# Loading most constants after the first norm's factor, and a lower limit on the work issued ahead of a step, in a decoder trunk on one core

## The chip, the core and the metric

The kernel runs on one core of a Trainium2 chip. A core has a matrix engine (TensorE, PE in the profile, with its weight loads as PEld), three engines for elementwise work (VectorE, DVE; ScalarE, ACT; GpSimd, POOL), and SyncE (SP), which here only issues transfers. Each engine has a queue of its own and works through it in order; engines wait for one another by semaphores. Transfers (DMAs) are issued by SyncE, ScalarE or GpSimd and then run beside the engines.

The metric is the device time of one execution in microseconds (us). The kernel before takes 902.55 us, the median of three runs.

## What is computed

Two layers of a hybrid decoder trunk over 256 rows of 2048 numbers, in 32-bit floats. Each layer normalises its rows, multiplies them by one wide matrix, feeds four groups of heads, gates their outputs, and multiplies the result by an output matrix; a last norm ends the whole.

```python
def hybrid_layer(x, layer_idx, ...):
    h = rms_norm(x, norm_g)
    p = split_columns(jnp.einsum("bsd,de->bse", h, w_in))
    fox = forgetting_attention(...) * silu(p["fox_g"])      # softmax with a forget gate
    diff = rms_norm(differential_attention(...)) * silu(p["diff_g"])
    moba = moba_attention(...) * silu(p["moba_g"])
    gla = rms_norm(gla_chunked(...)) * silu(p["gla_g"])     # gated linear attention
    mixed = jnp.concatenate([fox, diff, moba, gla], axis=-1)
    return x + jnp.einsum("bse,ed->bsd", mixed, w_out)

def reference(x, ...):
    for l in range(DEPTH):                                  # DEPTH = 2
        x = hybrid_layer(x, l, ...)
    return rms_norm(x, final_norm_g)
```

`rms_norm` multiplies each row by 1/rms, the reciprocal root of the mean of its squares. It is the same factor for a whole row, so the kernel multiplies the rows without it first and puts the factor on the product.

## The kernel before

**Steps.** The work of TensorE is a list of steps, `plan`. A normal step multiplies both halves of the rows (2 x 128) by a slice of weights of two blocks of 128 rows, most often 512 columns wide. For accuracy each operand is split into a high part and a low part, and a step makes three products: high by high, low by high, high by low. So a normal step is 12 matmuls of 128x512, eight that need the weights' high part `hi` and four that need their low part `lo`. Eight steps make a block (a product of one column range), whose sum lies in two banks of PSUM until ScalarE or VectorE takes it out. Two of the wide products are made with fewer matmuls out of sums and differences of halves: these are the pair steps (`"pair"`), six matmuls each, some of which read sums of the normalised rows that the task `sum_forms` prepares on VectorE. They stand between the normal steps of blocks 3 to 12 of each layer.

**The loop.** The last part of `hybrid_trunk` goes over `plan` and writes every engine's queue in one order. For step i it:

- calls the results of blocks that are complete (`settle`, which calls `done`), as soon as 1/rms of the layer is known (`("r", l)` in `ready`) and a buffer is free;
- emits the high part of step i+3 on ScalarE (`prepare`);
- emits the matmuls of step i (`multiply`, `multiply_form`);
- calls `tick`, which emits other work, and
- emits the low part of step i+3 on VectorE (`complete`). SyncE then loads weights into the buffer `raw` that this frees; there are five.

There are four buffers each for `hi` and `lo`, so the parts of step i+4 wait for TensorE to have left step i.

**Other work.** Everything else (norms, attention, gates, transposes through memory and back) is written as Python generators in the list `tasks`. `tick` goes through them in the order of the list, lets each go on by up to three pieces, and stops as soon as VectorE's or ScalarE's planned end (`v_.tail`, `a_.tail`) lies more than `AHEAD` past TensorE's planned time (`times.now`). A planner, `Times` and `Timed`, keeps these: each operation of VectorE or ScalarE costs a fixed time and a time per element, a transfer made by `move` the number given with it, a transfer issued by a plain `dma_start` nothing. A task goes on only when its last result is planned within `LEAD`, 1.5 us. The planner orders the queues; it puts no waits into them. Where a step needs something that no task has emitted yet, `tick(False)` is called until it is there.

**The start.** Blocks 0 to 2 (columns of the gated linear group and a few others) are made in steps 0 to 23, chunk by chunk as the rows arrive. The generator `first_rms` squares the four chunks on ScalarE, sums them on VectorE, has TensorE sum over partitions (a matmul by `one`, side<-one,four in the profile, after step 20) and, in the same piece, emits `pw` on VectorE and the power on GpSimd that gives 1/rms (`rstd`). `know_rows` then gives out `("r", 0)`, `settle` calls `gla_first` for block 0, and only after this the high part of step 24 is emitted.

The task `constants` starts when the last chunk of rows is split. It issues all constants' loads on ScalarE's queue: `ct` (tables), the small gate matrix (`gla_wa2`, `gla_ba`, into `w3`, split into `wa`), the masks, `neg_b` (the causal mask), `gng`, `fb`, the lambdas (`lamt`) and `dng`. After them come the cast of the masks on VectorE, the split of `wa` and the products of the lambdas. `gla` waits for the key "constants".

**The end of a layer.** The groups' products go into `mTh` and `mTl` (high and low part; the profile shows `mTl<-four,mTh`), which the output projection reads group by group: the first two groups for three ranges of columns, then the third group, then the fourth.

Line 265 of the profile is the helper that emits every operation of VectorE and ScalarE, line 440 the one that emits matmuls; so groups are told apart by their tiles.

## Time and profile before

| | |
|---|---|
| runs | 902.55 us median of 3 (901.48 to 902.99) |
| the profiled execution's own time | 902.47 us |
| its span, first to last instruction | 900.7 us |
| TensorE idle in the span | 900.7 - 884.1 = 16.6 us |
| mean granted clock of TensorE | 0.996 |
| bytes moved | 227.44 MB, mean 253 GB/s |

The page's chain of work that ended last has TensorE for 88% of the span, ScalarE for 4%, transfers for 3%, VectorE for 2%. A row of the timeline gives start and length in us, engine and line, operation, the tile written and those read, the shape, how many instructions were merged, and in brackets how long the engine had been idle and what ended that. A `q` after an engine's name marks its queue: an instruction that issues a transfer or waits. A busy TensorE may still be slow; the granted clock in the view of windows tells.

### The profile page before, as it was taken

What the parts mean: (1) busy time and instruction counts of PE and PEld (TensorE: products, weight loads), DVE (VectorE), ACT (ScalarE), POOL (GpSimd) and SP (SyncE); (2) the same over time, 40 slices, a digit from 0 to 9 for tenths busy, and PEclk for the clock granted to TensorE, in tenths of its full rate; (3) what the DMA queues carried; (4) which work ended last, traced back from release to release, by engine and by line L of the source; (5) the groups of instructions that cost most, each with busy time, mean ns of one, the idle gap of its engine ahead of it and who ended that gap; (6) DMA issues with size and microseconds to landing.
All of it is one profiled execution on the core that took longest, in us unless ns stands there. A gap on an engine that the chain in (4) does not pass through costs nothing.

```text
span 900.7 us, 12457 instructions
## 1 busy us (share of the span) xinstructions
PE 884.1 (98%) x4380; PEld 751.8 (83%) x4380; DVE 662.3 (74%) x943; ACT 560.5 (62%) x846; POOL 61.7 (7%) x87
## 2 busy tenths in 40 slices
PE   9989999999999999999999989999999999999996
PEld 7977888988888888888899877898888888888886
DVE  6668989787776956666658868877767789376673
ACT  7568765686557656654746975567655476675461
POOL 1001100100010001000000010110000100011000
PEclk9999999999999999999999999999999999999999
DMA  8879987778696695887877896967959967859842
GB/s 294 280 210 304 295 245 232 239 225 320 214 277 228 230 326 158 283 311 231 280 241 274 280 317 198 255 187 294 305 200 279 286 198 226 306 186 322 327 145 95
DMA packets 84141, 227.44 MB, mean 253 GB/s; under 512 B 9979, under 2 KB 30443, under 8 KB 83950
## 3 DMA queue, kind: packets, MB, share of 16 engines
q1 hardware_dynamic: 73336, 192.00, 62.6%
q0 software_dynamic: 9152, 33.03, 14.3%
q10 hardware_dynamic: 1590, 1.62, 0.6%
q8 instruction: 34, 0.56, 0.2%
q14 instruction: 29, 0.24, 0.1%
HBM read 204.06 MB, written 22.55 MB: 252 GB/s over the span
## 4 chain that ended last, share of the span: by engine, by line
PE 88%; ACT 4%; DMA 3%; DVE 2%; issue 2%; SPq 0%; POOL 0%; POOLq 0%; DVEq 0%; ACTq 0%
PE mm L440 75%; PE side L440 13%; DMA raw<-in_weights 2%; ACT hi L265 1%; ACT L265 1%; DVE lo L265 1%; ACT four L265 1%; DVE four L265 1%; DVE tq L265 0%; DMA four<-in_xt 0%; DMA gng<-in_gla_norm_gt 0%; SPq L271 0%; ACT eight L265 0%; ACT mTh L265 0%; ACT fe L265 0%
## 5 line engine op out<-in xcount | busy, mean ns | idle before, releaser
L265 ACT ACTIVATE hi<-raw 128x1024 fp32r<-128x1024 f32 (+2 forms) x319 | 317.3, 1010 | 203.8 <-PE mm L440 118.0
L440 PE MATMUL mm<-hi,hTp 128*128 128x512 f32 (+1 forms) x1760 | 432.4, 382 | 5.3 <-ACT four L265 3.0
L265 DVE TENSOR_TENSOR lo<-raw,hi 128x1024 fp32r<-128x1024 f32 (+2 forms) x319 | 362.7, 1155 | 98.3 <-ACT hi L265 91.9
L440 PEld LDWEIGHTS mm<-hi,hTp 128*128 128x128 f32 x1760 | 323.3, 189 | 66.1 <-ACT hi L265 4.0
L440 PE MATMUL mm<-lo,hTp 128*128 128x512 f32 (+1 forms) x880 | 238.5, 381 | 3.0 <-DVE lo L265 3.0
L440 PEld LDWEIGHTS mm<-lo,hTp 128*128 128x128 f32 x880 | 162.4, 188 | 35.2 <-DVE lo L265 5.8
L440 PE MATMUL mm<-hi,mTh 128*128 128x512 f32 (+1 forms) x256 | 69.7, 379 | 0.0
L440 PE MATMUL mm<-hi,mTl 128*128 128x512 f32 (+1 forms) x256 | 69.0, 376 | 0.0
L440 PE MATMUL mm<-lo,mTh 128*128 128x512 f32 (+1 forms) x256 | 69.0, 376 | 0.0
L440 PEld LDWEIGHTS mm<-hi,mTl 128*128 128x128 f32 x256 | 46.3, 188 | 8.9
L440 PEld LDWEIGHTS mm<-lo,mTh 128*128 128x128 f32 x256 | 46.3, 188 | 8.9
L271 POOL DMA_DIRECT2D four<-far x40 | 21.9, 547 | 450.2 <-DVE lo L265 183.9
L440 PEld LDWEIGHTS mm<-hi,mTh 128*128 128x128 f32 x256 | 45.7, 188 | 8.0
L265 ACT ACTIVATE four<-mm,rstd 128x512 f32<-128x512 f32 (+2 forms) x56 | 36.6, 667 | 24.7 <-PE mm L440 24.4
L265 ACT ACTIVATE four<-four 128x512 fp32r<-128x512 f32 (+3 forms) x44 | 35.1, 816 | 16.6 <-DMA four<-far 12.1
L265 DVE STREAM_TRANSPOSE four<-four 128x1024 f32<-128x1024 f32 (+1 forms) x34 | 38.6, 1140 | 1.8 <-ACT four L265 1.8
L440 PEld LDWEIGHTS side<-four,four 128*128 128x128 f32 (+1 forms) x336 | 36.3, 190 | 2.5 <-issue 1.4
L440 PE MATMUL side<-four,four 128*128 128x128 f32 (+3 forms) x336 | 37.3, 281 | 0.0
L265 DVE TENSOR_TENSOR four<-four,four 128x512 fp32r<-128x512 f32 (+3 forms) x31 | 26.7, 883 | 9.2 <-ACT four L265 9.2
L271 POOL DMA_DIRECT2D xs<-in_weights x24 | 21.1, 879 | 177.3 <-DVE lo L265 60.2
L265 ACT ACTIVATE hi<-xs 128x1024 fp32r<-128x1024 f32 x24 | 25.4, 1058 | 8.7 <-PE mm L440 8.6
L265 DVE TENSOR_TENSOR lo<-xs,hi 128x1024 fp32r<-128x1024 f32 x24 | 29.1, 1214 | 0.5 <-ACT hi L265 0.4
(146 smaller groups left out, 674.2 us busy)
## 6 DMA issues: line engine op xcount, KB each, us to landing
raw<-in_weights SPq DMA_DIRECT2D x271, 512.0 KB, 5.2
four<-far POOLq DMA_DIRECT2D x34, 512.0 KB, 6.8
far<-four SPq DMA_DIRECT2D x128, 128.0 KB, 4.8
raw<-in_weights SPq DMA_DIRECT2D x46, 348.0 KB, 4.5
xs<-in_weights POOLq DMA_DIRECT2D x24, 512.0 KB, 7.5
xs<-in_weights SPq DMA_DIRECT2D x8, 512.0 KB, 7.1
xs<-in_x SPq DMA_DIRECT2D x4, 512.0 KB, 8.2
kept<-xs SPq DMA_DIRECT2D x1, 2048.0 KB
```

The source lines that it names most:

```text
L265: return f(*args, **kw)
L271: self.eng.dma_start(out, src, **kw)
L440: t_.matmul(out, lhsT, rhs, start=start, stop=stop, **kw)
```

## The change

Four constants change and two are new: `AHEAD` goes from 5.0 to 3.0, `ROOM` from 5.0 to 2.0; `BEFORE_LO` and `BEFORE_HI` are 1.5.

In `constants`, `ct` and the small gate matrix are loaded where they were, now with a planned time (4.5 and 5.0 us), and `wa` is split as soon as they are planned to be there. Then the task waits for `("r", 0)`. Only then are the masks loaded (planned 5.0 us), cast and given out under a key of their own, and then the lambdas, `dng`, `neg_b`, `gng` and `fb`. `gla` waits for "masks" after its scans.

In the loop, `tick` gets two limits, one for VectorE and one for ScalarE, in place of one for both and a `room` for ScalarE. `lasts(z)` is the planned length of step z. The limits are the length of the next two steps less 1.5 us, at most `AHEAD`, and for ScalarE at most `ROOM` at the last step of a block.

```diff
-AHEAD = 5.0
+AHEAD = 3.0
-ROOM = 5.0
+ROOM = 2.0
+BEFORE_LO = 1.5
+BEFORE_HI = 1.5
...
-            if v_.tail > times.now + AHEAD or a_.tail > times.now + ranks["room"]:
+            if v_.tail > times.now + ranks["v"] or a_.tail > times.now + ranks["a"]:
                 break
...
         yield from until(("h", 0, 3))
-        nc.scalar.dma_start(ct, const)
+        a_.move(ct, const, 4.5)
         w3 = s2.get([P, DEPTH, 256])
         g_.memset(w3, 0.0)
         for i in range(0, 96, 32):
             nc.scalar.dma_start(w3[i:i + 16], gla_wa2.rearrange("l r e -> r l e"))
-            nc.scalar.dma_start(w3[i + 16:i + 17].rearrange("p l e -> p (l e)"), gla_ba.rearrange("(o l) e -> o (l e)", o=1))
-        yield
+            a_.move(w3[i + 16:i + 17].rearrange("p l e -> p (l e)"), gla_ba.rearrange("(o l) e -> o (l e)", o=1), 5.0)
+        yield
+        hi_of(wa, w3)
+        yield
+        lo_of(wa[64:96], w3[64:96], wa[64:96])
+        s2.put(w3)
+        given_out("constants")
+        yield from until(("r", 0))
         c, n = CAT["masks"]
         mb = s4.get([P, n], BF16)
-        nc.scalar.dma_start(mb, const_b[:, c:c + n])
-        yield
+        a_.move(mb, const_b[:, c:c + n], 5.0)
+        yield
+        v_.tensor_copy(masks.rearrange("p l t -> p (l t)"), mb)
+        s4.put(mb)
+        given_out("masks")
+        lamt = s2.get([P, DEPTH, 4, 64])
+        a_.move(lamt.rearrange("p l a d -> p (l a d)"), bcast_rows(diff_lam, 0, DEPTH * 256), 5.0)
+        nc.scalar.dma_start(dng, diff_norm_gt)
         c, n = CAT["neg"]
         nc.scalar.dma_start(neg_b, const_b[:, c:c + n])
         nc.scalar.dma_start(gng, gla_norm_gt)
         nc.scalar.dma_start(fb.rearrange("p l h -> p (l h)"), bcast_rows(fox_fb, 0, DEPTH * H))
-        yield
-        lamt = s2.get([P, DEPTH, 4, 64])
-        nc.scalar.dma_start(lamt.rearrange("p l a d -> p (l a d)"), bcast_rows(diff_lam, 0, DEPTH * 256))
-        nc.scalar.dma_start(dng, diff_norm_gt)
-        yield
-        v_.tensor_copy(masks.rearrange("p l t -> p (l t)"), mb)
-        s4.put(mb)
-        hi_of(wa, w3)
-        yield
-        lo_of(wa[64:96], w3[64:96], wa[64:96])
-        s2.put(w3)
-        given_out("constants")
         yield
...
         s2.put(gl)
+        yield from until("masks")
         yield from until(("gla_qk", l))
...
+    def lasts(z):
+        return 1.36 if "pair" in z else len(z["kts"]) * (z["block"]["n"] + 32) / 400.0
...
-        ranks["room"] = ROOM if s["last"] else AHEAD
+        soon = sum(lasts(z) for z in plan[i + 1:i + ahead])
+        ranks["v"] = min(AHEAD, soon - BEFORE_LO)
+        ranks["a"] = min(AHEAD, soon - BEFORE_HI, ROOM if s["last"] else AHEAD)
         tick()
-        ranks["room"] = AHEAD
+        ranks["v"] = ranks["a"] = AHEAD
```

## The prediction

> **What bounds the kernel now.** I read the page first, for the share of each engine.

> ```profile
> span 900.7 us, 12457 instructions
> PE 884.1 (98%) x4380; PEld 751.8 (83%) x4380; DVE 662.3 (74%) x943; ACT 560.5 (62%) x846; POOL 61.7 (7%) x87
> ```

> TensorE is the bound: 16.6 us of the span are not its own (900.7 - 884.1), and no edit of this change removes a matmul. So the most that can be won is in the places where TensorE waits or runs slowly. The view of waits, for PE alone, names them:

> ```profile
> PE mm L440 <- DVE lo L265: 3.0, 4, 1.4
> PE mm L440 <- ACT four L265: 3.0, 2, 2.3
> PE mm L440 <- ACT hi L265: 2.2, 1, 2.2
> ```

> These are 8.2 us in seven waits: four for a step's low part, two for a bank that ScalarE had not emptied, one for a high part. The rest of the 16.6 us is mostly start and end. The busy time hides one more loss, which the view of windows shows beside the single wait for a high part:

> ```profile
> 58.50:61.00 2.50, 0.28 (x3) 0.00 (x1) 0.02 (x1) 2.49 (x6) 1.04 (x1) 1.00 0.80 213
> 61.00:65.00 4.00, 4.00 (x11) 3.13 (x12) 4.00 (x4) 4.00 (x9) 0.00 (x0) 0.57 0.95 217
> ```

> The columns are stage and length, then busy us of PE, PEld, DVE, ACT and POOL, the granted clock, the DMA share and GB/s. PE did nothing from 58.78 to 61.00, and then "busy" for 4.00 us at a clock of 0.57: 0.43 x 4.00 = 1.72 us lost. The wait and its slow restart cost 2.22 + 1.72 = 3.94 us. The timeline tells why the high part came late:

> ```profile
> 43.22 1.06 ACT L265 ACTIVATE hi<-raw 128x1024 fp32r<-128x1024 f32 x1 [2.17 <-PE side L440]
> 45.04 0.35 ACTq L552 DMA_DIRECT2D four<-in_const_b  x1
> 45.43 0.68 ACTq L555 DMA_DIRECT2D neg_b<-in_const_b  x1
> 46.64 0.33 ACTq L556 DMA_DIRECT2D gng<-in_gla_norm_gt  x1
> 47.01 0.44 ACTq L557 DMA_DIRECT2D fb<-in_fox_fb  x1
> 47.49 0.59 ACTq L560 DMA_DIRECT2D four<-in_diff_lam  x1
> 48.13 0.51 ACTq L561 DMA_DIRECT2D dng<-in_diff_norm_gt  x1
> 48.22 0.48 PE L440 MATMUL mm<-lo,hTp 128*128 128x348 f32 x2
> 48.69 1.06 ACT L265 ACTIVATE four<-four 128x1024 f32<-128x1024 f32 x1 [4.41 <-DMA gng<-in_gla_norm_gt]
> 51.12 1.44 ACT L265 ACTIVATE hi<-raw 128x696 fp32r<-128x696 f32 x2
> 51.53 0.58 PE L440 MATMUL side<-one,four 128*128 128x1 f32 x4
> 55.41 0.87 DVE L265 TENSOR_TENSOR lo<-raw,hi 128x696 fp32r<-128x696 f32 x1
> 56.20 0.15 DVE L265 TENSOR_SCALAR pw<-side 128x2 f32<-128x2 f32 x1
> 56.51 0.71 POOL L265 TENSOR_TENSOR rstd<-pw,halfpow 128x2 f32<-128x2 f32 x1 [52.80 <-DVE pw L265]
> 58.30 0.48 PE L440 MATMUL side<-lo,hTp 128*128 128x348 f32 x2
> 59.88 1.06 ACT L265 ACTIVATE hi<-raw 128x1024 fp32r<-128x1024 f32 x1
> 61.00 2.00 PE L440 MATMUL mm<-hi,hTp 128*128 128x512 f32 x4 [2.22 <-ACT hi L265]
> ```

> ScalarE is through with a high part at 44.28 and then issues six loads of constants until 48.64; only then comes the last square of the first norm (48.69), and behind it the high parts of steps 21 to 23. So the low part of step 23 is done at 56.28, the power's input `pw`, emitted behind it, at 56.35, and 1/rms at 57.22. The results of block 0 need 1/rms, stand ahead of step 24's high part on ScalarE, and that part ends at 60.94: TensorE, free since 58.78, starts at 61.00.

> **The change part by part.**

> *Constants after 1/rms.* The six issues (0.35 + 0.68 + 0.33 + 0.44 + 0.59 + 0.51 = 2.90 us, 4.36 us from 44.28 to 48.64 with their waits) leave that place; so do the cast of the masks and the work on the lambdas on VectorE. The seven loads of `ct` and `wa`'s source stay, ahead of the high part at 43.22, which waits for TensorE anyway. The square can then start at 44.3 instead of 48.69. What is late next? Step 23's high part needs the buffer of step 19, which TensorE leaves at 48.70 (48.22 + 0.48): it runs from 48.7 to 49.5, the low part until 50.4. `pw` also needs the matmul of the sums, which ends at 52.11 by its place between steps 20 and 21. So `pw` moves from 56.20 to about 52.2, and 1/rms from 57.22 to about 53.2. Step 24's high part ended 60.94 - 57.22 = 3.72 us after it; now at 56.9, ahead of 58.78 by 1.9 us. The wait of 2.22 us goes, and with it the slow clock: **-3.9 us**. Bounds: at least 0 (1/rms no earlier), at most these 3.94.

> What comes back: one load is issued a step later and five some 3.5 us after that (the planner now counts 5.0 us for them), between the high parts of steps 26 and 27. That puts 0.35 and 2.55 us into ScalarE's queue, ahead of the results of block 2 and of high parts. Its cover is this idle time, which shows that it had caught up:

> ```profile
> 67.71 1.06 ACT L265 ACTIVATE hi<-raw 128x1024 fp32r<-128x1024 f32 x1 [0.33 <-PE mm L440]
> 70.62 1.06 ACT L265 ACTIVATE hi<-raw 128x1024 fp32r<-128x1024 f32 x1 [1.85 <-DMA raw<-in_weights]
> ```

> That is 2.18 us against 2.90, with the high parts some 2 steps early, so I cost it at nothing; without the cover it is 0.7 us, and up to 3.6 us (48.64 - 45.04) if the issues wait again. The added waits: the cast of the masks waits on VectorE for its load, with the low part of step 26 queued behind it and TensorE behind that; `gla` waits for "masks" after its scans (85.06 below), long after the cast, at no cost. The loads of weights move too: SyncE issues one when a low part has freed its buffer, and so sooner wherever a low part comes sooner.

> At this place the clock is the larger unknown. The row shows that 2.22 us without matmuls were followed by a clock of 0.57. [...]

> *Work ahead limited.* Ticks emit other work until VectorE's or ScalarE's planned end is 5.0 us past TensorE's. Now it is 3.0 us, or less: two coming steps of 512 columns last 2.72 us each (5.44 - 1.5 = 3.94, so 3.0 holds), with a pair step among them 1.36 + 2.72 - 1.5 = 2.58, and ScalarE has 2.0 at a block's end. No instruction is added or removed; lows and highs come sooner in their queues, and the rest later. The longest of the four waits for a low part shows what it could do:

> ```profile
> 82.50 0.17 DVE L265 SCALAR_TENSOR_TENSOR fz<-fx,fe 128x8 f32<-128x8 f32 x1 [2.35 <-ACT fe L265]
> ...
> 83.92 1.22 DVE L265 TENSOR_TENSOR four<-four,hTp 128x1024 f32<-128x1024 f32 x1
> 85.06 1.36 DVE L265 TENSOR_TENSOR_SCAN four<-one,four 128x128 f32<-128x128 f32 x4
> 86.34 2.33 DVE L265 TENSOR_TENSOR lo<-raw,hi 128x1024 fp32r<-128x1024 f32 x2
> 87.59 0.73 PE L440 MATMUL mm<-lo,hTp 128*128 128x512 f32 x2 [1.43 <-DVE lo L265]
> ```

> VectorE idles 2.35 us for ScalarE, then does a sum and four scans (1.22 + 1.36) ahead of a low part that is 1.43 us late. A limit of 2.58 may send the scans behind that low part, 1.36 of the 1.43 us; the idle 2.35 us, a dependency that the planner times too early, remains. So I take half of the waits for low parts, 1.5 of 3.0 us: **-1.5 us**. Bounds: -6.0 (those and the waits for banks all gone) and +3.0 (as many new ones of the same size). The longer wait for a bank stays, since it hangs on a load:

> ```profile
> 531.73 1.06 ACT L265 ACTIVATE hi<-raw 128x1024 fp32r<-128x1024 f32 x1 [0.30 <-DMA raw<-in_weights]
> 532.69 1.25 ACT L265 ACTIVATE four<-mm,r0.125_4134 128x512 f32<-128x512 f32 x2
> 533.41 1.21 PE L440 MATMUL mm<-hi,hTp 128*128 128x512 f32 x4 [2.28 <-ACT four L265]
> ```

> *Sum*, against the profiled execution's own 902.47 us (span 900.7 and 1.8 around it; the median of the runs is 902.55, 0.1 more): 902.5 - 3.9 - 1.5 = **897.1 us**, rounded to 897.0.

> **The rivals.**

> *Only the early part counts.* The limits move waits about without reducing their sum. For it: the waits come from ScalarE's and the loads' real lateness, which the planner does not see. 902.5 - 3.9 = 898.6.

> [...]

> *The gain is handed on.* Everything runs 4 us earlier into a stage (80 to 85 us below) where ScalarE and the loads are full; five issues add 2.55 us and TensorE waits there instead. Against it: in 50 to 55 us the loads were nearly idle for want of low parts, so they can move up too.

> ```profile
> 50.00:55.00 5.00, 4.93 (x25) 3.79 (x24) 4.83 (x10) 2.56 (x4) 0.00 (x0) 1.00 0.31 83
> 80.00:85.00 5.00, 5.00 (x23) 4.01 (x23) 2.62 (x5) 4.97 (x6) 0.85 (x1) 1.00 1.06 407
> ```

> With 2.55 given back and the limits worth nothing: 902.5 - 3.9 + 2.55 = 901.1.

> *Slower: work held back misses the output projection.* Group products enter it in a fixed order, and the second and third groups come late:

> ```profile
> 383.74 1.23 DVE L265 TENSOR_TENSOR mTl<-four,mTh 128x1024 fp32r<-128x1024 f32 x1 [4.32 <-ACT mTh L265]
> 392.12 1.07 PE L440 MATMUL mm<-hi,mTh 128*128 128x512 f32 x4
> 402.49 1.23 DVE L265 TENSOR_TENSOR mTl<-four,mTh 128x1024 fp32r<-128x1024 f32 x1
> 410.80 1.07 PE L440 MATMUL mm<-hi,mTh 128*128 128x512 f32 x4
> ```

> They are ready 7.15 us (392.12 - 384.97) and 7.08 us (410.80 - 403.72) ahead. The limits hold back just this work. If a chain comes over 7.1 us later, TensorE waits; at 10 us, four times over two layers, 4 x 2.9 = 11.6 us: 902.5 - 5.4 + 11.6 = 908.7. Against it: the queues are not full all the time (VectorE 74%), and a shorter queue also lets a chain's next link start sooner.

> *The change does not do what it says*: 1/rms stays where it is, since `pw` stays behind the low part of step 23 for another reason (a load, or the constants' waits): 902.5 - 1.5 = 901.0.

> **How the numbers follow.** Chances: forecast 0.60, only the early part 0.13, slow clock 0.04, handed on 0.10, slower 0.08, 1/rms not earlier 0.05. The range reaches from 892.0 (3.9 and all 6.0 us gone is 892.6) to 902.0 (3.9 won, 3.0 lost to new waits, is 901.6). It leaves out the slower rival and the tails of the others, some 0.15. A difference of 0.2%, 1.8 us, is about what a measurement of this kernel can tell from none: faster is below 900.7. There lie the forecast, the two rivals near 898.7 and half of the one handed on: 0.82. Within: the other half and the last rival, 0.10. Slower: 0.08.

> **What would show it.** Right: in the changed profile ScalarE's square stands near 44.5, `pw` near 52.2, `rstd` ends near 53.2; no wait of PE for a high part at 58.8 and a granted clock of 1.00 in 61 to 65; the five issues stand after 60 us with no wait of PE within 5 us; PE's waits for low parts sum to about 1.5 us, those for banks still to some 3. Wrong: `rstd` near 57, or a wait between 60 and 90 us longer than 1.43; waits for a new cause after 100 us that add up to over 3 us; or the last `mTl` of a group within a step of its use.

## The result and the profile after

The changed kernel takes **906.93 us** (median of 9 runs, 904.77 to 910.15) against 902.66 us for the kernel before (9 runs, 900.64 to 903.50): a ratio of 1.0053, with a 95% interval of 1.0035 to 1.0071. The forecast was 897.0 us, with a range up to 902.0. It went the other way. The profiled span is 4.5 us longer (905.2 against 900.7).

The first lines of the page of the changed kernel (share of each engine), and then the view of waits for PE alone:

```profile
span 905.2 us, 12467 instructions
...
PE 885.9 (98%) x4380; PEld 752.4 (83%) x4380; DVE 662.6 (73%) x943; ACT 558.7 (62%) x846; POOL 60.4 (7%) x87
```

```profile
PE mm L442 <- ACT mTh L267: 5.2, 2, 2.9
PE mm L442 <- ACT hi L267: 3.1, 1, 3.1
PE mm L442 <- DVE lo L267: 1.8, 6, 0.4
...
PE mm L442 <- ACT hTp L267: 0.4, 1, 0.4
```

The number of matmuls is the same. Of the waits of before, those for low parts fell from 3.0 to 1.8 us, those for banks (3.0) and the one for a high part near 60 us (2.2) are gone. In their place stand two waits for `mTh`, the part of a group's result that enters the output projection, one for another high part, and a short one (0.4) for split rows (`hTp`) near the start. The view of windows shows the two places of the old loss and two new ones (columns as before):

```profile
61.00:65.00 4.00, 4.00 (x19) 3.31 (x18) 3.97 (x7) 3.00 (x4) 0.00 (x0) 1.00 0.87 313
...
390.40:393.80 3.40, 3.40 (x9) 2.43 (x8) 3.40 (x4) 3.40 (x6) 0.00 (x0) 0.51 0.42 159
...
540.60:544.00 3.40, 3.40 (x10) 2.62 (x9) 3.16 (x11) 3.40 (x9) 0.00 (x0) 0.50 0.52 186
```

The clock is full where it was 0.57. But behind two of the new waits it is halved for 3.40 us: 0.49 x 3.40 = 1.67 and 0.50 x 3.40 = 1.70 us lost.

**The account.** Won: the wait and the slow clock near 60 us (2.2 + 1.7), low parts 3.0 - 1.8 = 1.2, banks 3.0; together 8.1 us. Lost: `mTh` 5.2, a high part 3.1, slow clock 1.7 + 1.7; together 11.7. Net 3.6 of the 4.5 us by which the span grew. The wait for `hTp` adds 0.4, and the stretch from TensorE's last matmul to the end of the span another 0.4 (7.4 us before, 7.7 after), which leaves 0.1.

**The early part, step by step.** The timeline of the changed kernel, against the lines around 50 us shown in the prediction:

```profile
44.83 1.05 ACT L267 ACTIVATE four<-four 128x1024 f32<-128x1024 f32 x1
...
51.77 0.16 DVE L267 TENSOR_SCALAR pw<-side 128x2 f32<-128x2 f32 x1 [0.50 <-PE side L442]
...
52.08 0.70 POOL L267 TENSOR_TENSOR rstd<-pw,halfpow 128x2 f32<-128x2 f32 x1 [48.38 <-DVE pw L267]
...
55.45 1.07 ACT L267 ACTIVATE hi<-raw 128x1024 fp32r<-128x1024 f32 x1
...
58.27 1.08 PE L442 MATMUL mm<-hi,hTp 128*128 128x512 f32 x4
...
63.05 0.35 ACTq L273 DMA_DIRECT2D four<-in_diff_lam  x1
...
67.23 0.33 ACTq L571 DMA_DIRECT2D fb<-in_fox_fb  x1
...
102.75 0.61 PE L442 MATMUL mm<-hi,mTh 128*128 128x512 f32 x2
```

The square starts at 44.83 (48.69 before), `pw` at 51.77 (56.20), 1/rms ends at 52.78 (57.22), step 24's high part ends at 56.52 (60.94), and TensorE starts the step at 58.27 with no wait. The last five issues lie on ScalarE's queue between 63.05 and 67.56, which is 4.5 us with their waits; TensorE did not stop there. At the first pair step that multiplies by the sums TensorE is 6.4 us ahead of the kernel before:

```profile
109.16 0.62 PE L440 MATMUL mm<-hi,mTh 128*128 128x512 f32 x2
```

**Where it is lost.** The second group's results reach the output projection by a long chain: products on TensorE, results stored by SyncE and fetched by GpSimd, work of ScalarE and VectorE between them, at the end a scale by `dng` and the split into `mTh` and `mTl`. First the kernel before in the timeline: one set of products in the middle of the chain, the last products, the first matmul of the first group's projection (which belongs to TensorE's fixed order and serves as a mark), and `mTh`:

```profile
294.15 1.69 PE L440 MATMUL side<-four,four 64*128 64x256 f32 x24
...
349.86 1.59 PE L440 MATMUL side<-four,four 128*128 128x256 f32 x12
...
359.48 0.61 PE L440 MATMUL mm<-hi,mTh 128*128 128x512 f32 x2
...
382.64 1.06 ACT L265 ACTIVATE mTh<-four 128x1024 fp32r<-128x1024 f32 x1
```

The same in the changed kernel, with the two uses that waited:

```profile
294.25 1.69 PE L442 MATMUL side<-four,four 64*128 64x256 f32 x24
...
353.25 0.62 PE L442 MATMUL mm<-hi,mTh 128*128 128x512 f32 x2
...
358.69 1.60 PE L442 MATMUL side<-four,four 128*128 128x256 f32 x12
...
386.44 1.07 PE L442 MATMUL side<-lo,mTh 128*128 128x512 f32 x4
387.54 1.15 ACT L267 ACTIVATE four<-four,dng 128x1024 f32<-128x1024 f32 x1 [6.77 <-DMA four<-far]
388.71 1.06 ACT L267 ACTIVATE mTh<-four 128x1024 fp32r<-128x1024 f32 x1
389.82 1.57 PE L442 MATMUL mm<-hi,mTh 128*128 128x512 f32 x4 [2.31 <-ACT mTh L267]
...
838.78 1.20 PE L442 MATMUL mm<-hi,mTh 128*128 128x512 f32 x4 [2.85 <-ACT mTh L267]
```

TensorE passes the mark 6.2 us sooner (353.25 against 359.48), but the products of the middle are no sooner and the last ones 8.8 us later. Against the mark, the last products go from 9.6 us ahead of it (359.48 - 349.86) to 5.4 us behind it. `mTh` ends at 383.70 in the kernel before, 8.4 us ahead of its use at 392.12; here at 389.77, 2.3 us after TensorE was free (387.51). The chain has slipped by **10.7 us** against TensorE. Of this, TensorE's being earlier at the use is 4.6 us (392.12 against 387.51), and `mTh`'s being later is 6.1 us. The same wait comes in the second layer at 838.78.

The wait for a high part is of another kind. It lies some 90 us into the second layer, whose first product TensorE starts at 448.36. The timeline of the changed kernel there:

```profile
538.14 1.06 ACT L267 ACTIVATE four<-four 128x1024 f32<-128x1024 f32 x1 [5.07 <-DMA four<-far]
539.11 1.04 ACT L267 ACTIVATE hi<-raw 128x1024 fp32r<-128x1024 f32 x1
...
540.20 1.32 PE L442 MATMUL mm<-hi,hTp 128*128 128x512 f32 x3 [3.12 <-ACT hi L267]
```

The high part stands on ScalarE behind an operation that waited 5.07 us for a fetch; TensorE waits behind both. In the kernel before, the last operation of that form ahead of `four<-ct,dgs` waits for nothing and runs 13 us sooner:

```profile
524.73 1.04 ACT L265 ACTIVATE four<-four 128x1024 f32<-128x1024 f32 x1
```

In the kernel before TensorE stops a few steps ahead of this place, for the bank of 533.41 that the prediction shows (2.28 us, at full clock behind it). So 2.3 of the 3.0 us won at banks and the loss of 3.1 + 1.7 us at the high part belong to one stretch of the second layer, which as a whole lost.

### The profile page after: what moved, and what is told of

Same layout as the page of the kernel before. It is cut to its first block, busy times and chain, and to the rows that moved or that the text cites. A ratio compares the mean times of both kernels' runs of the same rounds, so it can differ in the third digit from the quotient of the medians.

```text
span 905.2 us, 12467 instructions
## 1 busy us (share of the span) xinstructions
PE 885.9 (98%) x4380; PEld 752.4 (83%) x4380; DVE 662.6 (73%) x943; ACT 558.7 (62%) x846; POOL 60.4 (7%) x87
## 4 chain that ended last, share of the span: by engine, by line
PE 81%; DMA 7%; DVE 5%; issue 5%; ACT 1%; POOL 0%; POOLq 0%; SPq 0%; ACTq 0%; DVEq 0%
PE mm L442 70%; PE side L442 11%; DMA four<-far 3%; DMA raw<-in_weights 2%; DVE lo L267 2%; DMA far<-four 1%; DVE four L267 1%; DVE mx L267 1%; DVE tq L267 0%; DVE mTl L267 0%; ACT hi L267 0%; ACT four L267 0%; ACT mTh L267 0%; DMA neg_b<-in_const_b 0%; DVE side L267 0%
## 5 line engine op out<-in xcount | busy, mean ns | idle before, releaser
L267 DVE TENSOR_TENSOR mTl<-four,mTh 128x1024 fp32r<-128x1024 f32 x16 | 19.5, 1220 | 17.7 <-ACT mTh L267 17.7
```

The costliest lines, as they stand in the source:

```text
L267: return f(*args, **kw)
```

## The experiments

Theory A, formed from these views: the limits of 3.0 us and less hold back the chains, and everything that was lost is lost there, while the constants' part brings what was forecast. Its first rival: the moved constants are the cause. The expectations name the theories and their numbers for each run. All times are medians in us; the ratio is to the kernel before in the same set of runs, over all of its runs and so not exactly that of two medians (902.34 for E1 to E4, 902.10 for E6, E7, E8 and E10, 902.65 for E11 to E13), with its 95% interval.

| run | what it is | time | ratio | interval |
|---|---|---|---|---|
| E1 | constants moved, old limits | 904.72 | 1.0036 | 1.0022 to 1.0051 |
| E2 | new limits, constants as before | 911.32 | 1.0090 | 1.0076 to 1.0104 |
| E3 | limit of 3.0 alone | 920.69 | 1.0215 | 1.0195 to 1.0236 |
| E4 | limit by coming steps alone | 913.14 | 1.0115 | 1.0097 to 1.0132 |
| E13 | ScalarE's 2.0 at a block's end alone | 913.16 | 1.0121 | 1.0100 to 1.0142 |
| E6 | new limits until step 59 only | 898.89 | 0.9958 | 0.9945 to 0.9971 |
| E7 | new limits from step 60 only | 915.02 | 1.0146 | 1.0125 to 1.0168 |
| E8 | E1, the sums given out one by one | 901.22 | 0.9989 | 0.9976 to 1.0002 |
| E10 | change, old limits in steps 100 to 151 | 898.19 | 0.9950 | 0.9938 to 0.9961 |
| E11 | change, old limits in steps 100 to 111 | 900.39 | 0.9983 | 0.9965 to 1.0000 |
| E12 | change, old limits in steps 122 to 151 | 913.94 | 1.0127 | 1.0107 to 1.0147 |

### E1 and E2: the two parts apart

E1 sets `AHEAD` and `ROOM` back and takes out the limit by coming steps:

```diff
-        soon = sum(lasts(z) for z in plan[i + 1:i + ahead])
-        ranks["v"] = min(AHEAD, soon - BEFORE_LO)
-        ranks["a"] = min(AHEAD, soon - BEFORE_HI, ROOM if s["last"] else AHEAD)
+        ranks["v"], ranks["a"] = AHEAD, ROOM if s["last"] else AHEAD
```

> The constants' part of the change alone; the limits on work ahead are those of before (5.0 us for both engines). Theory A (the lower limits stretch the chain of the second group, differential attention, until the output projection waits for it): TensorE's waits for mTh near 387 and 836 us are gone, the gain at 58 to 65 us stays, and the time is 895 to 898. Theory B (TensorE, being some 6 us earlier, outruns a chain that takes as long as before; the limits matter little): the waits for mTh stay, 4 to 6 us in sum, and the time is 903 to 907.

The waits for `mTh` are gone, as theory A has it, but the time, 904.72, is far above what it gave. Its timeline, and then its window at the longest wait:

```profile
108.57 4.19 DVE L267 TENSOR_TENSOR tq<-eight,four 64x128 f32<-64x128 f32 x14
112.77 1.22 DVE L267 TENSOR_TENSOR mTl<-four,mTh 128x1024 fp32r<-128x1024 f32 x1
113.91 1.50 DVE L267 TENSOR_TENSOR eight<-eight,four 128x128 f32<-128x128 f32 x7
115.33 1.22 DVE L267 TENSOR_TENSOR lo<-xs,hi 128x1024 fp32r<-128x1024 f32 x1
116.60 1.22 PE L442 MATMUL mm<-lo,mTh 128*128 128x512 f32 x2 [3.68 <-DVE lo L267]
```

```profile
116.60:120.00 3.40, 3.40 (x8) 2.72 (x9) 3.34 (x6) 1.06 (x1) 0.87 (x1) 0.51 0.41 70
```

VectorE works through 4.19 + 1.22 + 1.50 us of other work ahead of one low part; TensorE waits 3.68 us and then runs 3.40 us at a clock of 0.51. In the code this is the place where the first pair step finds the sums that it needs not yet planned: the loop then calls `tick(False)`, which moves the planned time on by 0.3 us a call, until all that is missing is emitted, and only then goes on to the step; so the limits no longer hold this work back. So theory A failed as to the constants: with the old limits, moving them makes the kernel slower.

E2 puts `constants` back as it was (and `gla` without the wait for "masks") and keeps the new limits:

```diff
         yield from until(("h", 0, 3))
-        a_.move(ct, const, 4.5)
+        nc.scalar.dma_start(ct, const)
...
-        yield from until("masks")
         yield from until(("gla_qk", l))
```

> The lower limits alone; the constants are loaded and used as before the change. Theory A: the chain of the second group ends three steps (8.2 us) later against TensorE, so the waits for mTh are there in both layers, and the wait near 58 us is back: 908 to 912. Theory B: no waits for mTh, since TensorE is no earlier than before: 901 to 903.

The time, 911.32, is within theory A's range. The view of waits of E2 (its profiled execution took 915.74 us, the longest of the five):

```profile
PE mm L442 <- ACT mTh L267: 5.9, 2, 3.9
```

The waits for `mTh` are there without any move of a constant: the moved constants don't cause them.

### E3, E4 and E13: the limits one at a time

E3 keeps `AHEAD = 3.0` alone (`ROOM = 5.0`, and no limit by coming steps):

```diff
-        soon = sum(lasts(z) for z in plan[i + 1:i + ahead])
-        ranks["v"] = min(AHEAD, soon - BEFORE_LO)
-        ranks["a"] = min(AHEAD, soon - BEFORE_HI, ROOM if s["last"] else AHEAD)
+        ranks["v"] = ranks["a"] = AHEAD
```

> The constants' part with the flat limit of 3.0 us alone: no limit from the coming steps, none of its own for ScalarE at a block's end. Theory A: the queues' order puts the second group's last parts five steps later than with 5.0 us, so the waits for mTh are longer than in the changed kernel: 6 us or more in each layer, 909 to 914. Theory B: as the changed kernel, 905 to 908.

E4 keeps the limit by coming steps alone (and issues `fb` together with the masks):

```diff
-AHEAD = 3.0
+AHEAD = 5.0
-ROOM = 2.0
+ROOM = 5.0
...
         a_.move(mb, const_b[:, c:c + n], 5.0)
+        nc.scalar.dma_start(fb.rearrange("p l h -> p (l h)"), bcast_rows(fox_fb, 0, DEPTH * H))
```

> The constants' part with the limit from the coming steps alone (two steps less 1.5 us, at most 5.0), and the load of fb issued with that of the masks. Theory A: the second group's last parts come four steps later than with a flat 5.0 us; waits for mTh of 3 to 5 us in each layer, 904 to 908. Theory B: as the changed kernel, 905 to 908, with the same waits for mTh.

E13 keeps `ROOM = 2.0` alone: `AHEAD = 5.0`, and the line `ranks["v"], ranks["a"] = AHEAD, ROOM if s["last"] else AHEAD` of E1.

> The constants' part with a limit of 2.0 us for ScalarE at a block's end alone, 5.0 us otherwise. Theory A: the second group's chain is emitted at the same steps as with a flat 5.0 us, so no waits for mTh; the sums for the pair steps are no sooner either, so a wait near 112 us as in the constants' part alone: 902 to 906. Theory B: as the changed kernel, 905 to 908 with waits for mTh.

The views of waits of E3, of E4 and of E13, in this order:

```profile
PE mm L442 <- ACT mTh L267: 14.7, 2, 7.7
```

```profile
PE mm L442 <- ACT mTh L267: 6.2, 2, 3.6
```

```profile
PE mm L442 <- DVE lo L267: 10.5, 10, 3.5
```

Either limit on all work ahead (3.0, or by the coming steps) is enough to make `mTh` late, once in each layer; ScalarE's limit at a block's end is not, and it has another loss, low parts late by 10.5 us in all, the longest near 121 us. All three are slower than expected. The expectations priced the wait that they were about; each kernel also emits its early work in another order and loses there in ways that were not traced one by one.

### E6 and E7: early or late

E6 adds to the changed kernel

```diff
+        if i >= 60:
+            ranks["v"] = ranks["a"] = 5.0
```

and E7 the same with `i < 60`.

> The constants' part, with the lower limits in steps 0 to 59 of the plan only and a flat 5.0 us from there on. Theory A (the constants' part is worth some 6 us up to 94 us; a flat 5.0 us then lets the sums for the pair steps come too late at step 42, where all that is still missing is emitted at once, ahead of low parts; lower limits prevent that, and cost only where they stretch the second group's chain): no wait over 1 us between 60 and 180 us, no wait for mTh, 895 to 899. Theory B (each reordering makes waits of about the same sum somewhere): 902 to 907, with waits at other places.

> The constants' part, with a flat 5.0 us in steps 0 to 59 and the lower limits from there on. Theory A: both losses, the waits of 1.3 and 3.8 us near 100 and 112 us that the constants' part alone had, and the waits for mTh in both layers of the changed kernel: 909 to 914. Theory B: 902 to 907.

E6 takes 898.89, within theory A's range and 3.2 us less than the kernel before, with no wait for `mTh`. E7 takes 915.02, a microsecond above theory A's range, and has them again. Its view of waits:

```profile
PE mm L442 <- DVE lo L267: 6.6, 8, 3.6
PE mm L442 <- ACT mTh L267: 4.8, 2, 2.7
```

So the limits help in the first 60 steps and harm behind them. In the first 60, E6 has no wait like the 3.68 us of E1, while the low part that is 3.6 us late in E7 stands near 116 us, as in E1; that the low limits do this by letting the sums be emitted in time is argued, not shown.

### E8: what made E1 slow

E8 is E1 with each group's sums given out by itself, and each pair step needing only its own:

```diff
-            plan.append({**z, "need": {("h", l, c) for c in range(4)} | ({("forms", l)} if z["form"] in SUM_OF else set())})
+            plan.append({**z, "need": {("h", l, c) for c in range(4)} | ({("forms", l, SUM_OF[z["form"]])} if z["form"] in SUM_OF else set())})
...
+            given_out(("forms", l, f))
```

> The constants' part alone with the limits of before (5.0 us), but each of the four sums for the pair steps is given out as soon as it is split, and a pair step needs only its own; so nothing is emitted at once at step 42. Theory A: the wait of 3.8 us near 112 us and its slow clock go, 897 to 901. Theory B (VectorE and the loads are simply full between 75 and 130 us, whatever the order): the wait moves, 903 to 907.

901.22 is just outside the expected range. That is 3.5 us less than E1 in another set of runs (ratios 0.9989 and 1.0036), and no more than even with the kernel before. The timeline of E8 at the place of E1's wait:

```profile
109.12 2.37 DVE L267 TENSOR_TENSOR tq<-eight,four 64x128 f32<-64x128 f32 x8
111.52 1.23 DVE L267 TENSOR_TENSOR lo<-xs,hi 128x1024 fp32r<-128x1024 f32 x1
```

The low part now stands behind 8 of the 14 products of sums and not behind what follows them. The wait of 3.68 us is gone. So work forced ahead of a low part was what E1 lost there. The kernel before with its sums given out singly was not run, so how much of the 0.9 us by which E8 is ahead belongs to the constants is not known.

### E10, E11 and E12: which links of the chain

Each adds one condition to the changed kernel, in E10 as below, in E11 with 112 and in E12 with 122 to 152:

```diff
+        if 100 <= i % 172 < 152:
+            ranks["v"] = ranks["a"] = 5.0
```

(172 steps make a layer.)

> The changed kernel with a flat 5.0 us in steps 100 to 151 of each layer, the stretch in which the second group's chain is emitted; the rest as changed. Theory A: its last parts come three steps sooner, the waits for mTh near 387 and 836 us go (2.5 and 3.0 us and the slow clock after the first, some 7 us), the rest stays: 898 to 902. Theory B: the waits for mTh stay, since a transfer of 8 us stands in the chain: 905 to 908.

> The changed kernel with a flat 5.0 us in steps 100 to 111 of each layer alone, where the second group's chain waits for its first products. Theory A (the chain is stretched because a tick that finds a queue over its limit emits nothing, and the first two of the three lost steps are lost there): its last parts come two steps (5.4 us) sooner, more than the waits of 2.5 and 3.0 us, so both waits for mTh go: 898 to 902. Theory B (the stretch lies behind the products, in the softmax and the transposes): the waits for mTh stay, 905 to 908.

> The changed kernel with a flat 5.0 us in steps 122 to 151 of each layer alone, behind the second group's products. Theory A: what was lost ahead of the products is not made up, the waits for mTh stay or grow, 905 to 911. Theory B: they go, 898 to 902.

The timelines of E10, E11 and E12, in this order:

```profile
345.39 1.59 PE L442 MATMUL side<-four,four 128*128 128x256 f32 x12
...
355.01 0.62 PE L442 MATMUL mm<-hi,mTh 128*128 128x512 f32 x2
...
378.50 1.06 ACT L267 ACTIVATE mTh<-four 128x1024 fp32r<-128x1024 f32 x1
...
387.65 1.07 PE L442 MATMUL mm<-hi,mTh 128*128 128x512 f32 x4
```

```profile
350.98 1.59 PE L442 MATMUL side<-four,four 128*128 128x256 f32 x12
...
355.16 0.62 PE L442 MATMUL mm<-hi,mTh 128*128 128x512 f32 x2
...
383.02 1.04 ACT L267 ACTIVATE mTh<-four 128x1024 fp32r<-128x1024 f32 x1
...
387.80 1.07 PE L442 MATMUL mm<-hi,mTh 128*128 128x512 f32 x4
```

```profile
354.31 1.59 PE L442 MATMUL side<-four,four 128*128 128x256 f32 x12
355.75 0.63 PE L442 MATMUL mm<-hi,mTh 128*128 128x512 f32 x2
...
392.80 1.06 ACT L267 ACTIVATE mTh<-four 128x1024 fp32r<-128x1024 f32 x1
...
393.91 1.65 PE L442 MATMUL mm<-hi,mTh 128*128 128x512 f32 x3 [5.33 <-ACT mTh L267]
```

| us ahead (+) or late (-) | before | changed | E10 | E11 | E12 |
|---|---|---|---|---|---|
| last products against the mark | +9.6 | -5.4 | +9.6 | +4.2 | +1.4 |
| end of `mTh` against its use | +8.4 | -2.3 | +8.1 | +3.7 | -5.3 |

(For the kernels that wait, the lower row is less the wait.) E10 and E11 are within theory A's ranges; E12 went the way that it said, and further. With the old limits in steps 100 to 151 the chain is back where it was, to the tenth of a microsecond at its last products, and TensorE waits neither there nor in the second layer. E10 has the lowest median of this study, **898.19 us**, 0.9950 of the kernel before; E6 (0.9958) is within its interval. E11 shows that twelve steps at the chain's beginning are enough to take the wait away, though the low limits behind them still cost 4.7 us of the 8.4. E12 shows the reverse only in part. With the beginning late, the old limits in the later steps do bring the last products 6.8 us forward against the mark (from -5.4 to +1.4), but the waits for `mTh` don't go: from the start of the last products to the end of `mTh` it takes 39.6 us (354.31 to 393.86), against 31.1 in the changed kernel, and `mTh` is later than with the change alone. Why this last part is longer is open.

## Why the prediction failed

**What bounds the kernel**: right. All that was won or lost shows in TensorE's waits and in the slow clock behind them.

**Constants after 1/rms, -3.9**: the mechanism was right to half a microsecond (`pw` 51.77 for 52.2, end of `rstd` 52.78 for 53.2, the high part 56.52 for 56.9), and the wait and its slow clock are gone. But "comes back: nothing" was judged only by the next few microseconds. The last five issues took 4.5 us of ScalarE's queue where 2.55 were counted, with no wait of TensorE, as said. What came back stood 50 us further on: TensorE is early at the pair steps, the sums are not, and with the old limits (E1) it costs 3.68 us and a halved clock (0.51 in 116.60 to 120.00). Alone the part costs 2.4 us (904.72 against 902.34); with the sums given out singly it comes to 0.9 us less than before (E8), which the interval doesn't tell from nothing. With the new limits in place it is worth about what was forecast: by the ratios the changed kernel (1.0053) is 3.3 us ahead of E2 (1.0090). So its worth depends on the limits, where the sum added the two parts as if each stood alone.

**Slow clock stays, 898.8, given 0.04** (the wait of 2.2 us goes, the slow clock behind it does not): fell. No run shows a slow clock that comes at that place without a gap; the changed kernel's granted clock is 1.00 in 61 to 65 us once the gap is gone. In its place the runs show short gaps followed by a slow clock: 2.22 us by 0.57 in the kernel before (61 to 65 us), and 2.31 us by 0.51 in the changed one (390.40 to 393.80).

**Work ahead limited, -1.5, bounds -6.0 to +3.0**: this is the step that failed. Alone the limits cost 8.1 us by the ratio (E2), far outside the bound of +3.0. Its gain at the places that waited was there: low parts -1.2 and banks -3.0, where "the longer wait for a bank stays" was said; but for the longer one a wait for a high part came a few steps on. Its cost was bounded by "as many new ones of the same size", that is by waits at places that wait already. Two of the three longer new waits came where `mTh` had been ready 8.4 us (first layer) and 8.1 us (second) ahead of its use (the prediction, going by `mTl`, counted 7.15), and they alone are 5.2 us. Two of the three also carry a price that the bound left out, the halved clock (1.7 us each).

**The slower rival, 908.7, given 0.08**: this is what happened, in its mechanism; that its time also came near is luck, since the parts of its sum differ. The chain slipped 10.7 us where the point of decision was put at 7.1 and the priced slip at 10. It happened at two places (the second group in both layers) and not four; the waits 5.2 us and a clock loss of 1.7 made 6.9 us, not 11.6; the wait for a high part with its clock, 4.8 us, of which that rival says nothing, filled most of the gap. The argument against it failed: "the queues are not full all the time (VectorE 74%), and a shorter queue also lets a chain's next link start sooner". From the last products to the end of `mTh` that does hold (31.1 us against 33.8 before). But ahead of them the chain has many links, and in the code a call of `tick` that finds one queue over its limit emits nothing until the next step. What counts for a link is whether the queue is over the limit at the one moment when it is asked, not its mean share. A step of 512 columns is 2.72 us (392.12 to 394.84 in the kernel before), so a slip of 10.7 us is some four lost turns. That the links were lost this way was read from the code and fits E10 to E12; no run emptied a single link.

**Open.** The wait for a high part some 90 us into the second layer (3.1 to 4.4 us) is in the changed kernel, E2, E7 and E10 to E12, and with 1.3 us in E3; all have low limits there. The kernel before, E1, E6 and E8, which have the old ones, and E13 wait near that place for a bank instead, 1.8 to 2.3 us; so does E4, 3.6 us, though its limit is low. Which store or fetch the limits hold back there was not tried. E10 still has the wait (3.1 us, and some 1.7 for the clock behind it); with the bank's 2.2 us of E6 in its place, an estimate of what is left to win there is 2 to 3 us.

**The others.** Only the early part (898.6), gain handed on (901.1) and 1/rms not earlier (901.0) did not occur as such; the second came closest in E1, by another cause.

## What to carry to other kernels

A limit on work ahead acts on every chain of dependent work: before it is lowered, take each chain's slack at its use, divide it by the length of a step, and ask how many links may lose a turn; a mean engine share doesn't answer this. Limits belong to stages: here the low one pays in the first 60 steps (E6) and the old one where the chain runs (E10), and both kernels that divide them so beat the kernel before and the changed one. And when an early stage gets faster, look for the next place that needs something which has not become faster, however far off it is.

## What was not expected of the hardware

Counted off in lengths of 3.413 us from these starts, the gap of 2.31 us falls into one length, and so do 2.99 of the 3.12 us, while a border at 837.6 cuts the gap of 2.85 us into 1.66 and 1.19. In the kernel before, the gap of 2.22 us falls into one length, and the one of 2.28 us is cut into 1.0 and 1.3. So in these five gaps the halved clock goes with the idle time within one length, not with the length of the gap. Five gaps are few: how much idle time is enough, and whether the same holds elsewhere, is not shown.

Five DMA issues on ScalarE's queue took 4.5 us from the first to the last, where six had taken 3.6 us at the old place. Themselves the five lasted 0.33 to 0.45 us each, 1.9 us in sum, so more than half of the 4.5 us was waiting between them.
